# Loads of a mixture-of-experts layer: every second weight tile of the later experts issued from ScalarE's queue

## The chip, the cores and the metric

The kernel runs on one core of a Trainium2 chip. The metric is the device time of one execution in microseconds (us). TensorE (PE) multiplies, VectorE (DVE) and ScalarE (ACT) do elementwise work, GpSimd (POOL) does little here, and SyncE (SP) computes nothing: it issues loads and stores. ACT issues a few small loads as well. Each engine takes its instructions strictly in order, and a load is such an instruction: if its semaphores aren't there yet, all that stands behind it on that engine waits too.

## The reference, cut to what matters

One layer over 256 tokens of width 2048: a projection, two recurrent branches, a gated merge and a layer norm, then a mixture of experts in which each of 16 experts picks its 32 best tokens, and a second layer norm.

```
aff = softmax(h @ w_router)                       # 256 x 16
gate, idx = top_k(aff.T, 32)                      # per expert
xe  = h[idx]                                      # 16 x 32 x 2048
hid = silu(xe @ w1) * (xe @ w3)                   # w1, w3: 16 x 2048 x 1024
eo  = (hid @ w2) * gate                           # w2: 16 x 1024 x 2048
out = layer_norm(alpha * h + scatter_add(idx, eo))
```

All is float32. The three expert weights are 16 x 3 x 8 MB, each read once.

## The kernel before, in words

**Stages.** The projections and recurrences come first and are laid out by hand in one long interleaved order. The experts follow in four groups of four (`for gq in range(4)`, L1454). For each expert of a group PE runs the up product: 16 tiles of w1 and w3, taken in pairs, each tile 128 partitions x 2048 floats, which is 1 MB (L1469). ACT and DVE then form silu times gate: two ACT instructions on the result (L1479, L1480), four on DVE, four PE transposes (L1487) and one ACT copy (L1489), which writes the tile `hid`. After the fourth expert the down product runs over 32 tiles of w2, four (one per expert) for each of eight blocks of rows (L1518). At its end four `eo` copies on ACT (L1525), each behind the last matmul of its quarter of the columns, feed a product that scatters the rows back (L1528) and is added up on DVE. In the last group the final two blocks of rows are cut by columns into five stripes of 4 tiles, three of 512 KB a tile and two of 256 KB. Each group but the first begins with a gather: PE picks the tokens (L1388), DVE and ACT write them, half and half (L1395, L1393).

**The order of the loads.** The list `order` holds all 396 weight tiles in the order of their use: per group 64 of w1 and w3, then those of w2. `prefetch()` issues the next one, and `take()` hands out the next one. Tile 64 is the first w2 tile of the first group. The first 24 tiles are loaded early, into whatever buffers are free. From tile 24 on the buffers go round in a cycle of 18: nine `ring_a`, two `t8b`, seven `ring`. A tile's buffer is thus free when the tile some 18 places earlier has been multiplied.

**What sets the order of instructions.** Up to the end of the first expert (`region.close()`, L1474) it is as written. Behind that a scheduler places each engine's instructions by its own model of times. It also gives each load one of eight completion semaphores in turn (DMAHW0 to 7), over all engines together. A load first waits for the load that had the same semaphore before it, that is, for the one eight places earlier in the order in which loads were placed. So at most eight weight loads are under way at a time. In the kernel before all of these loads stand on SP (L135).

Of the kernel before, what the change touches and what calls it, by code (L numbers as in the profile page):

```python
# [54 lines left out]
def build(tc, x, w_in, gla_a_up_f, gla_a_bias_f, gla_a_up_b, gla_a_bias_b, gla_norm_g,  # L55
# [3 lines left out]
    nc = tc.nc  # L59
# [26 lines left out]
    def S(shape, tag, bufs=1, dt=F32):  # L86
        return (mid if tag in ("t8", "t8b", "x16") else sp if tag in main_tags else cp).tile(shape, dt, tag=tag, name=tag, bufs=bufs)
# [23 lines left out]
    def prefetch(halves=False):  # L111
        i = len(issued)
        if i < len(first):
            slot = first[i]
            i = use.index(slot) + first[:i].count(slot)
        else:
            slot = again[(i - len(first)) % len(again)]
        ap = order[i]
        shape = list(ap.shape)
        if slot == "a":  # L120
            t = ring_a[0].tile(shape, F32, tag="ring_a", name="ring_a", bufs=NRA)
        elif slot == "x":
            if not pair:
                both = S([128, 2, 2048], "x16", 2)
                pair.extend((both[:, 0], both[:, 1]))
            t = pair.pop(0).rearrange("p (k f) -> p k f", k=shape[1])
        elif slot == "t":
            t = S(shape, "t8b", 2)
        elif slot == "p":
            t = ring_p[0].tile(shape, F32, tag="ring_p", name="ring_p", bufs=NRP)  # L130
        else:
            t = ring_b[0](shape)
        issued[i] = t
        if not halves:
            nc.sync.dma_start(t, ap)  # L135
            return None
        n = shape[1] // 2
        nc.sync.dma_start(t[:, 0:n], ap[:, 0:n])
        return lambda: nc.sync.dma_start(t[:, n:], ap[:, n:])

    def take():
        while taken[0] not in issued:
            prefetch()
        taken[0] += 1
        return issued[taken[0] - 1]
# [1110 lines left out]
    def all_chains():  # L1256
# [38 lines left out]
        chain_pool.close()  # L1295
        ring_a.append(st.enter_context(tc.tile_pool(name="ra", bufs=1, side="left", reuse_waits="tile")))
        early.extend([lambda: prefetch(True)] * NRA)
        yield from load_y(0, "x16", 2)
        yield from merge_t()

    run_chain(all_chains())
    early.extend([lambda: prefetch(True)] * (NRX + NRT))
    need("out4")
    while early:
# [291 lines left out]
```

## Time and profile before

| | |
|---|---|
| median of 3 runs | 1819.86 us (1819.25 to 1820.95) |
| the profiled execution | 1819.94 us |
| its span, first to last instruction | 1818.2 us |
| PE busy | 88% of the span |
| DVE, ACT busy | 43%, 30% |
| mean granted TensorE clock | 0.962 |

Shares over the whole span mix two stages. In the first, up to about 850 us, PE, DVE and ACT are all busy; in the second, the experts, the DMA engines are. A row of the sliced view has 40 digits or numbers, one for each 45.5 us.

### The profile page before, as it was taken

To read this page: it belongs to the slowest core of one execution; us is meant where nothing else is said; L and a number is where in the kernel's file an instruction comes from. 1 tells how busy PE (TensorE), PEld (TensorE's weight loads), DVE (VectorE), ACT (ScalarE), POOL (GpSimd) and SP (SyncE) were. 2 spreads that over 40 slices of the span, in tenths; PEclk is the share of its full clock that TensorE was granted. 3 is DMA by queue.
4 is the path that set the end of the run, shared out by engine and by line. 5 is a ranking of instruction groups with operands and counts; after the bars stand their busy time and mean duration, and the time that the engine had idled before them with its cause. 6 is when DMAs were issued, how large, how long until landed. Compare 5 with 4: busy or idle time off the path is not lost.

```text
span 1818.2 us, 27708 instructions
## 1 busy us (share of the span) xinstructions
PE 1600.9 (88%) x11255; PEld 955.3 (53%) x11255; DVE 773.4 (43%) x1400; ACT 548.6 (30%) x1081; POOL 16.5 (1%) x42
## 2 busy tenths in 40 slices
PE   8999999999999999999776997668986679966696
PEld 8998897798777788889421232112331113411132
DVE  6778776777568866655321211111031110111104
ACT  5566454564566755444200000000010000100001
POOL 0000000000000000000000000000000000000000
PEclk9999999999999999999899999889999899998998
DMA  7757374654655668887999999999999999999997
GB/s 215 236 165 196 106 196 118 180 145 137 176 180 174 191 192 287 301 294 255 399 414 420 420 421 420 421 421 421 421 420 421 421 420 421 421 420 420 411 413 249
DMA packets 203113, 561.84 MB, mean 309 GB/s; under 512 B 49804, under 2 KB 100422, under 8 KB 156522
## 3 DMA queue, kind: packets, MB, share of 16 engines
q1 hardware_dynamic: 185008, 557.70, 81.8%
q10 hardware_dynamic: 17978, 2.37, 0.8%
q8 instruction: 88, 1.44, 0.3%
q14 instruction: 39, 0.32, 0.0%
HBM read 543.24 MB, written 16.78 MB: 308 GB/s over the span
## 4 chain that ended last, share of the span: by engine, by line
DMA 40%; PE 39%; DVE 5%; ACT 2%; issue 1%; SPq 0%; ACTq 0%; DVEq 0%
DMA ring<-in_w_dram 18%; DMA ring_a<-in_w_dram 17%; PE mm L284 7%; PE mm L285 6%; PE mm L286 6%; PE mm L1518 5%; DMA t8b<-in_w_dram 4%; PE mm L1469 2%; PE mm L275 2%; PE mm L277 1%; PE mm L276 1%; PE ax L1170 1%; DVE wlo L65 1%; DVE t L65 1%; ACT whi L238 1%
## 5 line engine op out<-in xcount | busy, mean ns | idle before, releaser
L65 DVE TENSOR_TENSOR wlo<-wraw,whi 128x512 fp32r<-128x512 f32 (+2 forms) x480 | 310.9, 664 | 179.1 <-ACT whi L238 173.4
L238 ACT ACTIVATE whi<-wraw 128x512 fp32r<-128x512 f32 (+2 forms) x480 | 283.8, 609 | 147.1 <-PE mm L286 61.1
L275 PE MATMUL mm<-x,whi 128*128 128x256 f32 x688 | 206.9, 301 | 2.9 <-ACT whi L238 2.9
L1469 PE MATMUL mm<-ring_a,x 128*32 128x512 f32 x776 | 156.0, 675 | 55.9 <-DMA ring_a<-in_w_dram 55.9
L277 PE MATMUL mm<-x,wlo 128*128 128x256 f32 x688 | 194.4, 283 | 0.8 <-issue 0.8
L276 PE MATMUL mm<-x,whi 128*128 128x256 f32 x688 | 194.7, 283 | 0.0
L1481 DVE TENSOR_SCALAR sig<-sig 64x512 f32<-64x512 f32 x16 | 6.8, 424 | 433.9 <-ACT sig L1479 433.9
L1518 PE MATMUL mm<-ring_a,hid 128*32 128x512 f32 (+1 forms) x524 | 164.0, 598 | 1.3 <-ACT sig L1479 1.3
L284 PE MATMUL mm<-whi,x 128*128 128x512 f32 x384 | 162.8, 424 | 0.0
L1469 PE MATMUL mm<-ring,x 128*32 128x512 f32 x592 | 117.5, 679 | 49.9 <-DMA ring<-in_w_dram 49.9
L285 PE MATMUL mm<-wlo,x 128*128 128x512 f32 x384 | 153.2, 399 | 0.0
L286 PE MATMUL mm<-whi,x 128*128 128x512 f32 x384 | 152.8, 398 | 0.0
L65 DVE TENSOR_TENSOR x<-x,ax 128x512 f32<-128x512 f32 (+1 forms) x34 | 22.2, 655 | 271.4 <-PE ax L1528 271.4
L275 PEld LDWEIGHTS mm<-x,whi 128*128 128x128 f32 x688 | 131.0, 190 | 12.3 <-issue 5.1
L276 PEld LDWEIGHTS mm<-x,whi 128*128 128x128 f32 x688 | 131.1, 191 | 2.9 <-issue 2.9
L1479 ACT ACTIVATE sig<-mm 64x512 f32<-64x512 f32 x16 | 9.4, 588 | 406.4 <-PE mm L1469 406.4
L277 PEld LDWEIGHTS mm<-x,wlo 128*128 128x128 f32 x688 | 131.0, 190 | 0.3 <-DVE wlo L65 0.3
L1518 PE MATMUL mm<-ring,hid 128*32 128x512 f32 x392 | 125.3, 594 | 1.3 <-ACT sig L1479 0.7
L1469 PEld LDWEIGHTS mm<-ring_a,x 128*32 128x32 f32 x776 | 30.1, 116 | 158.1 <-DMA ring_a<-in_w_dram 105.9
L1518 PEld LDWEIGHTS mm<-ring_a,hid 128*32 128x32 f32 x524 | 46.6, 111 | 111.2 <-issue 95.1
L1525 ACT ACTIVATE eo<-mm 128x512 f32<-128x512 f32 (+1 forms) x17 | 9.7, 572 | 294.2 <-PE mm L1518 281.3
L1469 PEld LDWEIGHTS mm<-ring,x 128*32 128x32 f32 x592 | 22.7, 117 | 133.0 <-DMA ring<-in_w_dram 92.3
(348 smaller groups left out, 2134.6 us busy)
## 6 DMA issues: line engine op xcount, KB each, us to landing
ring_a<-in_w_dram SPq DMA_DIRECT2D x180, 1024.0 KB
ring<-in_w_dram SPq DMA_DIRECT2D x139, 1024.0 KB
wraw<-in_w_in_dram SPq DMA_DIRECT2D x112, 512.0 KB
t8b<-in_w_dram SPq DMA_DIRECT2D x39, 1024.0 KB
wraw<-in_w_in_dram SPq DMA_DIRECT2D x96, 256.0 KB
wraw<-in_w_out_dram SPq DMA_DIRECT2D x24, 512.0 KB
ring_a<-in_w_dram SPq DMA_DIRECT2D x22, 512.0 KB
wraw<-in_w_up_rwkv_dram SPq DMA_DIRECT2D x16, 512.0 KB
```

The lines of the kernel that those rows point to most:

```text
L65: dve.tensor_tensor(out_, a, b, op=op)
L238: act(hi, raw, AF.Copy)
L275: mm(o, whi[:, sl], hi(k), start=(st0 and cb % 2 == 0), stop=False, skip_group_check=True)
L276: mm(o, whi[:, sl], lo(k), start=False, stop=False, skip_group_check=True)
L277: mm(o, wlo[:, sl], hi(k), start=False, stop=st1, skip_group_check=True)
L284: mm(o, hi(k)[:, sl], whi, start=st0, stop=False)
L285: mm(o, hi(k)[:, sl], wlo, start=False, stop=False)
L286: mm(o, lo(k)[:, sl], whi, start=False, stop=st1)
L1170: mm(pv[:, h, j, :], ke[:, h, j * 128:j * 128 + 128], qe[:, h, iq * 128:iq * 128 + 128], start=True, stop=True)
L1469: mm(ps[32 * q:32 * q + 32, :], xe[:, kb, e4 * 32:e4 * 32 + 32], wt[q // 2][:, k, (q % 2) * 512:(q % 2) * 512 + 512], start=(kb == 0), sto ...
L1518: mm(pss[c // 512][32 * e4:32 * e4 + 32, c % 512:c % 512 + m], hids[e4][:, fb % 4, fb // 4, :], wt[e4][:, j, c - c0:c - c0 + m], start=(fb ...
L1525: act(eo[:, 0:m], pss[c // 512][:, c % 512:c % 512 + m], AF.Copy)
```

## The change

From tile 64 on, a tile with an odd number is issued by ACT instead of SP. These are 166 of the 332 loads from there. All first loads, the small ones and the stores stay where they were.

```
         issued[i] = t
         if not halves:
-            nc.sync.dma_start(t, ap)
+
+            (nc.scalar if i >= 64 and i % 2 else nc.sync).dma_start(t, ap)
             return None
```

The new blank line moves all lines behind it by one (L1479 becomes L1480). As the scheduler places the rest, it also changes the order of loads and a few matmuls. In the rows below a tile has its buffer's name and a serial number; what a row waits for stands in brackets, and the same number on two engines is the same tile.

**ACT, end of the first group.** Before: the last three experts' instructions, and the four `eo` copies of the down product.

```order
L1489 ACTIVATE hid_10962<-ax_10957 128x256 [waits PE_49]
L1479 ACTIVATE sig_11061<-mm_10964 64x512 [waits DVE_49,PE_49]
L1480 ACTIVATE h1_11062<-mm_10964 64x512
L1489 ACTIVATE hid_11074<-ax_11069 128x256 [waits PE_49]
L1479 ACTIVATE sig_11173<-mm_11076 64x512 [waits DVE_49,PE_49]
L1480 ACTIVATE h1_11174<-mm_11076 64x512
L1489 ACTIVATE hid_11186<-ax_11181 128x256 [waits PE_49]
L1525 ACTIVATE eo_11418<-mm_11222 128x512 [waits PE_49]
L1525 ACTIVATE eo_11426<-mm_11223 128x512 [waits PE_49]
L1525 ACTIVATE eo_11434<-mm_11224 128x512 [waits PE_49,Activation_49]
L1525 ACTIVATE eo_11442<-mm_11225 128x512 [waits PE_49,Activation_49]
```

Now, from the same `hid_11074` on:

```order
L1490 ACTIVATE hid_11074<-ax_11069 128x256 [waits PE_49]
L136 DMA t8b_11252<-in_w2_dram 128x2048 [waits DMAHW3_49,DMAHW5_49,DMAHW1_49,DMAHW7_49,DMAHW0_49,PE_49]
L136 DMA ring_11256<-in_w2_dram 128x2048 [waits DMAHW5_49,DMAHW7_49,DMAHW0_49,PE_49]
L136 DMA ring_a_11228<-in_w2_dram 128x2048 [waits DMAHW3_49]
L1480 ACTIVATE sig_11173<-mm_11076 64x512 [waits DVE_49,PE_49]
L1481 ACTIVATE h1_11174<-mm_11076 64x512
L136 DMA ring_a_11232<-in_w2_dram 128x2048 [waits DMAHW5_49,DMAHW1_49]
L1490 ACTIVATE hid_11186<-ax_11181 128x256 [waits PE_49]
L136 DMA ring_11276<-in_w2_dram 128x2048 [waits DMAHW1_49]
L136 DMA ring_11280<-in_w2_dram 128x2048 [waits DMAHW3_49]
L136 DMA ring_11300<-in_w2_dram 128x2048 [waits DMAHW5_49,Activation_49]
L136 DMA t8b_11352<-in_w2_dram 128x2048 [waits DMAHW7_49,PE_49]
```

Tile 69 (`t8b_11252`) and tile 71 (`ring_11256`) stand before tile 65 (`ring_a_11228`), and tile 67 (`ring_a_11232`) between two of the expert's steps; tile 87 (`t8b_11352`) comes ahead of tile 79, which is the row behind the last. Tile 87 takes the buffer of tile 69 and so waits for PE.

**SP, the same place.** Before, tiles 64 to 72 in the order of use:

```order
L135 DMA ring_a_11226<-in_w2_dram 128x2048 [waits DMAHW0_49]
L135 DMA ring_a_11228<-in_w2_dram 128x2048 [waits DMAHW1_49]
L135 DMA ring_a_11230<-in_w2_dram 128x2048 [waits DMAHW2_49]
L135 DMA ring_a_11232<-in_w2_dram 128x2048 [waits DMAHW3_49]
L135 DMA ring_a_11250<-in_w2_dram 128x2048 [waits DMAHW4_49]
L135 DMA t8b_11252<-in_w2_dram 128x2048 [waits DMAHW5_49]
L135 DMA t8b_11254<-in_w2_dram 128x2048 [waits DMAHW6_49]
L135 DMA ring_11256<-in_w2_dram 128x2048 [waits DMAHW7_49,PE_49]
L135 DMA ring_11274<-in_w2_dram 128x2048 [waits DMAHW0_49,PE_49]
```

Now, from tile 64 (`ring_a_11226`) on:

```order
L136 DMA ring_a_11226<-in_w2_dram 128x2048 [waits DMAHW2_49]
L136 DMA ring_a_11230<-in_w2_dram 128x2048 [waits DMAHW4_49]
L136 DMA ring_a_11250<-in_w2_dram 128x2048 [waits DMAHW6_49]
L136 DMA t8b_11254<-in_w2_dram 128x2048 [waits DMAHW7_49]
L136 DMA ring_11274<-in_w2_dram 128x2048 [waits DMAHW0_49,PE_49]
L136 DMA ring_11278<-in_w2_dram 128x2048 [waits DMAHW2_49,PE_49]
L136 DMA ring_11298<-in_w2_dram 128x2048 [waits DMAHW4_49,PE_49]
L136 DMA ring_a_11302<-in_w2_dram 128x2048 [waits DMAHW6_49,PE_49]
L136 DMA t8b_11370<-in_w2_dram 128x2048 [waits DMAHW7_49,DMAHW0_49,PE_49]
L136 DMA ring_a_11322<-in_w2_dram 128x2048 [waits DMAHW2_49]
L136 DMA ring_11374<-in_w2_dram 128x2048 [waits DMAHW4_49,PE_49]
L136 DMA ring_a_11326<-in_w2_dram 128x2048 [waits DMAHW6_49]
```

The even tiles are left. From tile 78 (`ring_a_11302`) on near and far ones alternate: 78, 88, 80, 90, 82. Each far one waits for PE to have used the tile whose buffer it takes.

**ACT, between two experts of the second group.** `ring_11705` is the last tile of its second expert, and `sig_11715` the first step behind that expert's matmuls. Before: no load stands here.

```order
L1479 ACTIVATE sig_11603<-mm_11450 64x512 [waits PE_49]
L1480 ACTIVATE h1_11604<-mm_11450 64x512
L1489 ACTIVATE hid_11616<-ax_11611 128x256 [waits PE_49]
L1479 ACTIVATE sig_11715<-mm_11618 64x512 [waits DVE_49,PE_49]
L1480 ACTIVATE h1_11716<-mm_11618 64x512
L1489 ACTIVATE hid_11728<-ax_11723 128x256 [waits PE_49]
```

Now:

```order
L136 DMA ring_11693<-in_w3_dram 128x2048 [waits DMAHW6_49]
L136 DMA ring_11705<-in_w3_dram 128x2048 [waits DMAHW0_49]
L136 DMA ring_11733<-in_w3_dram 128x2048 [waits DMAHW2_49]
L136 DMA ring_11745<-in_w3_dram 128x2048 [waits DMAHW4_49]
L1480 ACTIVATE sig_11715<-mm_11618 64x512 [waits DVE_49,PE_49]
L1481 ACTIVATE h1_11716<-mm_11618 64x512
L136 DMA ring_a_11757<-in_w3_dram 128x2048 [waits DMAHW5_49]
L136 DMA ring_a_11769<-in_w3_dram 128x2048 [waits DMAHW7_49]
L1490 ACTIVATE hid_11728<-ax_11723 128x256 [waits PE_49]
L136 DMA ring_a_11781<-in_w3_dram 128x2048 [waits DMAHW1_49]
L136 DMA ring_a_11793<-in_w3_dram 128x2048 [waits DMAHW3_49]
L136 DMA t8b_11805<-in_w3_dram 128x2048 [waits DMAHW5_49]
```

At `sig_11715` four loads have been issued in a row, two of them for the next expert; two more stand between its steps.

**ACT, the last stripes.** Before, the five `eo` copies stand together:

```order
L1525 ACTIVATE eo_13627<-mm_13463 128x512 [waits PE_49]
L1525 ACTIVATE eo_13657<-mm_13464 128x512 [waits PE_49]
L1525 ACTIVATE eo_13687<-mm_13465 128x512 [waits PE_49,Activation_49]
L1525 ACTIVATE eo_13717<-mm_13466 128x256 [waits PE_49,Activation_49]
L1525 ACTIVATE eo_13745<-mm_13466 128x256 [waits PE_49,Activation_49]
```

Now:

```order
L1526 ACTIVATE eo_13627<-mm_13463 128x512 [waits PE_49]
L136 DMA ring_a_13673<-in_w2_dram 128x2x512 [waits DMAHW1_49]
L136 DMA ring_a_13677<-in_w2_dram 128x2x512 [waits DMAHW3_49]
L1526 ACTIVATE eo_13657<-mm_13464 128x512 [waits PE_49]
L136 DMA ring_a_13703<-in_w2_dram 128x2x256 [waits DMAHW5_49]
L136 DMA ring_a_13707<-in_w2_dram 128x2x256 [waits DMAHW7_49]
L136 DMA t8b_13731<-in_w2_dram 128x2x256 [waits DMAHW1_49]
L136 DMA ring_13735<-in_w2_dram 128x2x256 [waits DMAHW3_49,DMAHW2_49]
L1526 ACTIVATE eo_13687<-mm_13465 128x512 [waits PE_49,Activation_49]
L1526 ACTIVATE eo_13717<-mm_13466 128x256 [waits PE_49,Activation_49]
L1526 ACTIVATE eo_13745<-mm_13466 128x256 [waits PE_49,Activation_49]
```

The odd tiles of the third stripe wait behind the `eo` copy of the first, those of the last two stripes behind that of the second.

## Rows read from the trace of the kernel before

**Rows 1.** The page's slices: DMA engines' busy tenths, and GB/s moved.
```profile
DMA  7757374654655668887999999999999999999997
GB/s 215 236 165 196 106 196 118 180 145 137 176 180 174 191 192 287 301 294 255 399 414 420 420 421 420 421 421 421 421 420 421 421 420 421 421 420 420 411 413 249
```

**Rows 2.** Windows: length, busy by engine, clock, DMA share, GB/s in the last column.
```profile
880.00:900.00 20.00, 15.51 (x107) 8.73 (x108) 6.80 (x18) 2.29 (x5) 0.00 (x0) 0.76 1.01 417
940.00:960.00 20.00, 11.95 (x67) 2.24 (x65) 2.35 (x2) 1.07 (x2) 0.00 (x0) 1.00 1.01 424
1000.00:1700.00 700.00, 564.78 (x2545) 164.06 (x2543) 96.36 (x111) 34.52 (x70) 0.00 (x0) 0.94 1.01 421
```

**Rows 3.** The chain that ended last, two of its pieces: start, length, what.
```profile
1015.61 19.92 DMA ring_a<-in_w_dram
...
1115.50 19.85 DMA ring_a<-in_w_dram
```

**Rows 4.** What SP waited for, 1000 to 1700 us: total, times, longest.
```profile
SPq L135 <- DMA ring_a<-in_w_dram: 292.0, 139, 3.1
SPq L135 <- DMA ring<-in_w_dram: 230.1, 109, 3.1
...
SPq L135 <- PE mm L1518: 1.4, 5, 0.3
```

**Rows 5.** SP at line L135: ns of one issue (min/median/max), start times.
```profile
L135 SPq DMA_DIRECT2D ring_a<-in_w_dram x140: 327/328/328, 1013.1 to 1698.4; - x140
```

**Rows 6.** SP's timeline: start, length, queue, loads merged; one cycle of buffers.
```profile
1057.96 20.26 SPq L135 DMA_DIRECT2D ring_a<-in_w_dram  x9
...
1102.78 20.54 SPq L135 DMA_DIRECT2D ring_a<-in_w_dram  x9
```

**Rows 7.** ACT's timeline, end of group one, an expert of group two.
```profile
997.70 0.59 ACT L1479 ACTIVATE sig<-mm 64x512 f32<-64x512 f32 x1 [33.69 <-PE mm L1469]
...
1004.27 0.38 ACT L1489 ACTIVATE hid<-ax 128x256 f32<-128x256 f32 x1 [5.50 <-PE ax L1487]
1076.61 1.33 ACT L1525 ACTIVATE eo<-mm 128x512 f32<-128x512 f32 x2 [71.95 <-PE mm L1518]
...
1117.44 0.59 ACT L1479 ACTIVATE sig<-mm 64x512 f32<-64x512 f32 x1 [15.57 <-PE mm L1469]
1117.93 0.58 ACT L1480 ACTIVATE h<-mm 64x512 f32<-64x512 f32 x1
1124.02 0.38 ACT L1489 ACTIVATE hid<-ax 128x256 f32<-128x256 f32 x1 [5.51 <-PE ax L1487]
```

**Rows 8.** PE's timeline around the first down product, and the end of an expert.
```profile
995.75 1.91 PE L1469 MATMUL mm<-ring_a,ring 128*32 128x512 f32 x12 [1.44 <-DMA ring_a<-in_w_dram]
...
1004.17 7.50 PE L1429 MATMUL ax<-lnrow,ident 16*128 16x512 f32 x14
1011.59 1.07 PE L1518 MATMUL mm<-ring_a,hid 128*32 128x512 f32 x2
...
1024.04 11.50 PE L1518 MATMUL mm<-ring,hid 128*32 128x512 f32 x50
...
1115.48 1.91 PE L1469 MATMUL mm<-ring,x 128*32 128x512 f32 x12 [1.35 <-DMA ring<-in_w_dram]
```

**Rows 9.** A window in the last group, where ACT loads rows of ln2.
```profile
1720.00:1735.00 15.00, 14.70 (x55) 4.55 (x55) 7.34 (x9) 4.66 (x8) 0.00 (x0) 1.00 0.96 367
```

**Rows 10.** What ACT waited for, 1700 to 1760 us: a small load's landing.
```profile
ACT sig L1507 <- DMA h<-in_ln_b_dram: 5.1, 3, 2.1
```

**Rows 11.** The tail on ACT: first, second and last `eo` copy of five.
```profile
1783.90 0.60 ACT L1525 ACTIVATE eo<-mm 128x512 f32<-128x512 f32 x1 [48.26 <-PE mm L1518]
1789.29 0.60 ACT L1525 ACTIVATE eo<-mm 128x512 f32<-128x512 f32 x1 [4.79 <-PE mm L1518]
...
1801.23 0.38 ACT L1525 ACTIVATE eo<-mm 128x256 f32<-128x256 f32 x1 [2.31 <-PE mm L1518]
```

**Rows 12.** The tail on SP: its last weight load.
```profile
1792.83 0.37 SPq L135 DMA_DIRECT2D ring<-in_w_dram  x1
```

**Rows 13.** DMA queues, 1000 to 1818 us: packets, MB, share of 16 engines.
```profile
q1 hardware_dynamic: 51168, 335.03, 99.3%
...
q10 hardware_dynamic: 40, 0.04, 0.0%
```

## The prediction

> **What bounds the kernel now.** The sliced view comes first. From the 20th slice on, about 865 us, the DMA engines are at nine tenths or more and move 399 to 421 GB/s until the last slices [rows 1]. A window says it more sharply: from 1000 to 1700 us they move 421 GB/s at a share of 1.01, while PE is busy for 565 of 700 us [rows 2]. At that rate a 1 MB tile (1.049 MB) takes 2.49 us. SP's timeline agrees: the same nine buffers come round after 1102.78 - 1057.96 = 44.82 us, and 44.82 / 18 tiles = 2.49 us [rows 6]. The chain of waits consists of pieces of 19.85 to 19.92 us, each from a load's issue to its landing [rows 3]. That is 8 x 2.49 = 19.9, so eight loads are always under way, as many as there are semaphores. SP waits 292 and 230 us for such landings, but 1.4 us for the down product's matmuls [rows 4], so a tile's buffer is free well before its turn.
>
> Two things do not bound it. One issue takes SP 0.328 us [rows 5], 13% of the 2.49. And PE is quicker than the loads: when it had tiles in store it did 50 matmuls of the down product in 11.50 us, 0.23 each, so four, one tile, take 0.92 us [rows 8]. The experts' time is bytes over rate, and then a tail. The change can act in three ways only: by another rate, by leaving the DMA engines without work, or in the tail.
>
> **The change part by part.**
>
> *Issuing.* 166 issues of 0.328 us, 54 us in all, move to ACT. ACT mostly waits (33.69 us before one expert's first step, 71.95 us before the first `eo`) [rows 7], and SP does not need the relief. I take 0.
>
> *Rate.* The 332 loads from tile 64 on hold 335.5 MB (335.03 on SP's queue q1 from 1000 us on, almost the same stretch) and 0.04 MB on ACT's queue q10 [rows 13]. 335.5 / 421 is 797 us. Two queues with large loads at once stand nowhere in this trace. The nearest rows are full windows of one queue: the best, 424 GB/s, gives 791.3 us (-5.6), the worst, 417, gives 804.6 (+7.7) [rows 2]. I take 421, the 700 us that the change is made in: 0.
>
> The Trainium skill speaks against a gain here: "DMA: Bandwidth & Descriptors", section "Rules for kernel authors", says that spreading loads over several issuing engines does not help bandwidth, since all of them run on the same 16 DMA engines, and only saves issue time. By that rule this term is 0. The share of 1.01 with one queue agrees with it; that two queues move no more, no run here shows yet.
>
> *ACT behind PE, between experts.* ACT now stands at `sig_11715` with its next loads behind it, until PE has used that expert's last tile, `ring_11705`. From that landing on: 1.91 us of matmuls [rows 8], then the two ACT steps of 0.59 and 0.58 us [rows 7], some 3.3 us with what lies between, until ACT issues again. The next block, at the expert's `hid`, lasts until 1124.02 - 1117.44 = 6.6 us after the first step [rows 7], and two loads are issued before it. Under way beyond `ring_11705` are the two of ACT that stand ahead of `sig_11715` and SP's own, about four of the eight: 6 x 2.49 = 14.9 us of work against 3.3. Covered: 0. SP's loads hide it, and where SP is stopped too the cover ends.
>
> *The start of the down product, where both can stop.* SP stands at tile 88 until PE has used tile 70, ACT at 87 until PE has used 69. Before, tile 63 had landed at 995.75 and PE came back to the down product at 1011.59, after 7.50 us of broadcasts from 1004.17 on [rows 8]. Now tiles 69 and 71 are loaded out of turn, ahead of 65. That makes 64 and 65 up to 2 x 2.49 = 5.0 us late, and PE's return too: 1016.6. Tiles 64 to 71 then take 8 x 0.92 = 7.4 us, so both queues move again by 1024. With 64 landing at 995.75 + 3 x 2.49 = 1003.2, the twelve loads after it up to 78 (69 and 71 are done) last until 1003.2 + 12 x 2.49 = 1033. Margin 9 us: 0. Later in each down product a far tile goes ahead of a near one, 2.49 us of delay each time, which PE makes up at 0.92 us a tile.
>
> *Gathers.* ACT's eight gather steps now stand between loads that wait for landings, so PE follows the loads in a group's first expert instead of catching up in one go. 18 buffers less 8 under way leave 10 tiles, 25 us, of room: 0.
>
> *The ln2 rows.* From 1720 to 1735 us the rate is 367 [rows 9]: 15 x (1 - 367/421) = 1.9 us are lost already, because ACT's small loads take semaphores in the same turn and wait for ACT's steps. With weight loads between them this can go (-1.9) or happen twice more (+3.8). I take 0, the row as it is.
>
> *Tail.* The third stripe's odd tiles follow the first `eo` (1783.90) and those of the last two the second (1789.29) [rows 11]. Four issues of 0.33 behind a copy of 0.60 end at 1789.29 + 0.60 + 1.3 = 1791.2, before SP's last issue of today, 1792.83 [rows 12]. So the loads are not later. But far before near also holds here, and one tile of 512 KB out of turn puts the first copies back by 1.25 us; PE has more left to do when the last piece lands. Bounds 0 and +5.0 (one stripe of 2.1 MB at 421); I take +1.5, near one piece.
>
> Sum: 1819.94 + 1.5 = 1821.4, made against the profiled execution, which is 0.08 above the median of the runs. A change of this kernel under 0.2%, 3.6 us, can't be told from none.
>
> **The rivals.**
>
> *The queues run dry (slower).* The cover of 9 us at the down product fails: PE uses tiles 69 and 70 later than 1033, for instance because the two queues don't share evenly and tiles 65 and 67 come last. Then both queues stand, and a stop costs at least 2.1 us until a load lands again [rows 10] and 2.49 for its tile: 4.6 us. Four down products make 18.4, time 1839.8; if half of them are hit, 1830.6. For it: ACT is now tied to PE thirteen times by experts' steps and by four rounds of `eo`. Against: the covers above. It decides from a lag of PE of 9 us more than worked out.
>
> *Two queues move more (faster).* 424 GB/s instead of 421, and the loss at ln2 gone: 1821.4 - 5.6 - 1.9 = 1813.9. For it: single windows reach 424. Against: 1.01 of the DMA engines are busy as it is.
>
> The skill's ceiling, "DMA: Bandwidth & Descriptors", section "Where 436 GB/s comes from", is 435 GB/s; by it alone the 335.5 MB would take an estimated 771 us, 26 less. No window of this trace comes near it.
>
> *Two queues move less (slower).* 417 GB/s, as in the slowest full window: 1821.4 + 7.7 = 1829.1. Nothing in this trace speaks for it but that window.
>
> *The change does not act.* The order shows half of the loads on ACT, so this is out.
>
> **How the numbers follow.** Forecast 0.54, dry queues 0.22, more rate 0.15, less rate 0.09. The forecast's own spread, 1818.0 to 1828.7 (tail 0 to +5.0, ln2 -1.9 to +3.8), lies almost wholly within 3.6 us of the median, since both ends together are unlikely. So: faster 0.16, within 0.2% 0.53, slower 0.31. The range runs from 1813, just past the faster rival, to 1838, past the lower rate and most of the dry case.
>
> **What will show it.** Right: q10 carries 166 loads, 168 MB; from 1000 to 1700 us 420 to 422 GB/s; SP now waits for PE at some of its loads, and ACT for landings; PE's return to the first down product 1016 instead of 1011.6; the last `eo` 1 to 3 us later. Wrong: a stretch of the experts below 400 GB/s other than the ln2 rows (dry queues), or another rate all along (one of the two rate rivals).

## The result and the profile after

The changed kernel takes 1835.15 us (median of 4 runs, 1834.36 to 1836.11). The kernel before took 1820.03 us in the same session (4 runs). The ratio is 1.0083, with a 95% interval of 1.0070 to 1.0097: 15 us slower. That lies inside the forecast range. It is not the likeliest case of the prediction, which was "the same", but its first rival, the queues that run dry (1831 to 1840).

The slices come first, the line that answers to [rows 1]: DMA engines' busy tenths and GB/s in 40 slices of the span, and below it the two large queues over the whole program (packets, MB, share of 16 engines).

```profile
DMA  7857373745465668897999999999999999999996
GB/s 212 241 159 200 103 197 113 200 122 169 142 200 171 188 200 282 304 302 265 400 416 421 406 401 420 421 421 421 413 411 421 421 420 422 404 421 421 403 396 217
...
q1 hardware_dynamic: 159824, 389.92, 59.0%
q10 hardware_dynamic: 43162, 170.16, 23.1%
```

Before, every slice from the 22nd on stood at 420 or 421 until the last three. Now the row has dents (406, 401; 413, 411; 404), and between them it is back at 420 to 422. A rate that was lower all along would look different. Queue q10 now carries 170.16 MB, so the split took place.

Windows sharpen this (start and end; length, busy time of PE, of PE's weight loads, of DVE, ACT and GpSimd, granted clock, DMA share, GB/s). The first answers to [rows 2], the last two lie where [rows 9] does.

```profile
1000.00:1700.00 700.00, 488.56 (x2528) 134.41 (x2520) 98.08 (x112) 35.59 (x72) 0.00 (x0) 0.85 1.00 416
1020.00:1040.00 20.00, 19.04 (x106) 4.88 (x104) 3.69 (x6) 0.00 (x0) 0.00 (x0) 0.83 0.96 387
1080.00:1100.00 20.00, 20.00 (x120) 8.13 (x118) 6.07 (x10) 2.85 (x5) 0.00 (x0) 0.96 0.93 376
1320.00:1340.00 20.00, 19.62 (x98) 7.51 (x97) 5.88 (x9) 2.39 (x4) 0.00 (x0) 0.99 0.93 381
1720.00:1740.00 20.00, 12.06 (x67) 2.75 (x67) 5.60 (x5) 1.70 (x3) 0.00 (x0) 0.83 0.97 381
1740.00:1760.00 20.00, 19.27 (x69) 5.51 (x70) 3.89 (x8) 4.66 (x8) 0.00 (x0) 0.74 0.94 375
```

416 instead of 421 over 700 us is 700 x (1 - 416/421) = 8.3 us of DMA time. The dents lie at the start and the end of a down product (1020 and 1080 for the first group, 1320 for the end of the second; the slice with 404 holds the end of the third). The two windows at the ln2 rows lose 1.9 and 2.2 us against 421; before, 1720 to 1740 lost 1.9 and the next window, at 421, nothing.

What SP waited for from 1000 to 1700 us (total, times, longest) answers to [rows 4]:

```profile
SPq L136 <- DMA ring<-in_w_dram: 277.8, 51, 11.7
SPq L136 <- DMA ring_a<-in_w_dram: 216.7, 52, 9.1
SPq L136 <- PE mm L1519: 82.4, 8, 20.2
```

The third line is the news. SP waited 1.4 us for the down product's matmuls before; now 82.4 us, and 20.2 at a time, which is as long as eight loads take. The first such place, on three timelines (start, length, engine; idle time before and its releaser in brackets), ACT first:

```profile
1006.23 0.59 ACT L1480 ACTIVATE sig<-mm 64x512 f32<-64x512 f32 x1 [40.16 <-PE mm L1470]
...
1012.81 2.98 ACTq L136 DMA_DIRECT2D ring<-in_w_dram  x3
1032.15 0.36 ACTq L136 DMA_DIRECT2D t8b<-in_w_dram  x1
```

SP at the same place:

```profile
1013.30 0.33 SPq L136 DMA_DIRECT2D ring_a<-in_w_dram  x1
1032.19 0.33 SPq L136 DMA_DIRECT2D t8b<-in_w_dram  x1
```

And PE, which both wait for; its rows answer to [rows 8]:

```profile
1004.27 1.91 PE L1470 MATMUL mm<-ring_a,ring 128*32 128x512 f32 x12 [0.82 <-DMA ring_a<-in_w_dram]
...
1012.70 8.38 PE L1430 MATMUL ax<-lnrow,ident 16*128 16x512 f32 x14
1021.01 5.33 PE L1519 MATMUL mm<-ring_a,hid 128*32 128x512 f32 x8
1026.27 1.44 PE L1430 MATMUL ax<-lnrow,ident 16*128 16x512 f32 x2
```

From 1015.8 to 1032.15 neither queue issues anything. The loads under way finish, and the rate falls to 387. PE is 8.5 us later than before at the broadcasts (1012.70 against 1004.17), then takes 5.33 us for eight matmuls, and two more broadcasts follow. Only at 1032 has it used the tiles that the two queues stand at.

The tail on ACT, which answers to [rows 11]:

```profile
1796.65 0.60 ACT L1526 ACTIVATE eo<-mm 128x512 f32<-128x512 f32 x1 [37.42 <-PE mm L1519]
...
1804.51 0.60 ACT L1526 ACTIVATE eo<-mm 128x512 f32<-128x512 f32 x1 [7.26 <-PE mm L1519]
...
1815.08 0.38 ACT L1526 ACTIVATE eo<-mm 128x256 f32<-128x256 f32 x1 [2.31 <-PE mm L1519]
```

The last copy comes 13.85 us later than before (1801.23). From the first copy to the last it takes 18.4 us, before 17.3, so the tail itself grew by 1.1 us. The rest came earlier.

The part before the first expert's first step took between 906.5 and 918.4 us in the profiled runs below. Profiles are therefore also compared by the time from that step to the last copy. The step in the kernel before, then in the changed one:

```profile
912.37 0.59 ACT L1479 ACTIVATE sig<-mm 64x512 f32<-64x512 f32 x1
```

```profile
913.07 0.59 ACT L1480 ACTIVATE sig<-mm 64x512 f32<-64x512 f32 x1
```

1801.23 - 912.37 = 888.9 us before, 1815.08 - 913.07 = 902.0 after, 13.1 more.

### The profile page after: what moved, and what is told of

Same layout as the page of the kernel before. It is cut to its first block, busy times and chain, and to the rows that moved or that the text cites. A ratio compares the mean times of both kernels' runs of the same rounds, so it can differ in the third digit from the quotient of the medians.

```text
span 1832.6 us, 27555 instructions
## 1 busy us (share of the span) xinstructions
PE 1523.5 (83%) x11255; PEld 922.8 (50%) x11255; DVE 773.4 (42%) x1400; ACT 548.3 (30%) x1081; POOL 16.5 (1%) x42
## 3 DMA queue, kind: packets, MB, share of 16 engines
q10 hardware_dynamic: 43162, 170.16, 23.1%
## 4 chain that ended last, share of the span: by engine, by line
PE 41%; DMA 38%; DVE 5%; ACT 2%; issue 1%; ACTq 0%; DVEq 0%; SPq 0%
DMA ring_a<-in_w_dram 17%; DMA ring<-in_w_dram 15%; PE mm L285 7%; PE mm L286 6%; PE mm L287 6%; DMA t8b<-in_w_dram 5%; PE mm L1470 4%; PE mm L1519 3%; PE mm L276 2%; PE mm L278 1%; PE mm L277 1%; PE ax L1389 1%; PE ax L1529 1%; DVE sig L1483 1%; PE ax L1430 1%
## 5 line engine op out<-in xcount | busy, mean ns | idle before, releaser
L1470 PE MATMUL mm<-ring_a,x 128*32 128x512 f32 x776 | 139.6, 757 | 71.2 <-DMA ring_a<-in_w_dram 71.2
L1519 PE MATMUL mm<-ring_a,hid 128*32 128x512 f32 (+1 forms) x524 | 138.8, 634 | 26.2 <-DMA ring_a<-in_w_dram 25.6
L1519 PE MATMUL mm<-ring,hid 128*32 128x512 f32 x392 | 118.7, 623 | 32.4 <-DMA ring<-in_w_dram 32.4
L1480 ACT ACTIVATE sig<-mm 64x512 f32<-64x512 f32 x16 | 9.4, 588 | 356.7 <-PE mm L1470 233.3
L1470 PEld LDWEIGHTS mm<-ring_a,x 128*32 128x32 f32 x776 | 26.0, 125 | 152.4 <-DMA ring_a<-in_w_dram 111.1
L1519 PEld LDWEIGHTS mm<-ring_a,hid 128*32 128x32 f32 x524 | 33.4, 116 | 111.0 <-issue 71.3
```

The costliest lines, as they stand in the source:

```text
L1470: mm(ps[32 * q:32 * q + 32, :], xe[:, kb, e4 * 32:e4 * 32 + 32], wt[q // 2][:, k, (q % 2) * 512:(q % 2) * 512 + 512], start=(kb == 0), sto ...
L1519: mm(pss[c // 512][32 * e4:32 * e4 + 32, c % 512:c % 512 + m], hids[e4][:, fb % 4, fb // 4, :], wt[e4][:, j, c - c0:c - c0 + m], start=(fb ...
```

## The experiments

All ratios are to the kernel before, run on the same chip in the same session; the sections stand in the order in which the thinking went.

**Near first.** Each queue keeps its own loads in the order of the tiles; the split is unchanged.

```
-            (nc.scalar if i >= 64 and i % 2 else nc.sync).dma_start(t, ap)
+            q = int(i >= 64 and i % 2)
+            ins = (nc.scalar if q else nc.sync).dma_start(t, ap)
+            if i >= 64:
+                if q in last_load:
+                    follow(ins, last_load[q])      # order only, no semaphore
+                last_load[q] = ins
```

> The changed kernel, with one thing taken out: on each of the two queues the weight loads now stand in the order of their tiles, so that no load that must wait for a use by TensorE stands ahead of the load of a nearer tile. The loads are still split by halves between SyncE and ScalarE, and ScalarE's loads still stand behind its expert steps. Theory 'order' (far loads ahead of near ones stop both queues at once at the start and the end of a down product): the dips of the changed kernel at 1020-1040, 1080-1100, 1320-1340 (387, 376, 381 GB/s) go, SP's waits for the down product's matmuls (82.4 us) fall under 10 us, and the time is 1819 to 1824. Theory 'ScalarE is tied to TensorE' (its loads stand behind waits of its compute steps, whatever their order): the dips stay, SP's ring waits grow, 1830 to 1836. Theory 'two queues move less': below 420 GB/s in all windows and no lower than 1833. Tail and ln2 rows may keep 2 to 5 us in either of the first two.

Measured: 1829.58 us, ratio 1.0056 (1.0037 to 1.0074). Three windows, then SP's waits for the ln2 rows from 1000 us on, then two rows of ACT's timeline:

```profile
1000.00:1700.00 700.00, 494.35 (x2506) 135.46 (x2508) 98.01 (x112) 35.48 (x72) 0.00 (x0) 0.86 1.01 420
1720.00:1740.00 20.00, 15.63 (x71) 4.20 (x72) 6.37 (x6) 2.68 (x5) 0.00 (x0) 0.79 0.81 323
1740.00:1760.00 20.00, 18.16 (x76) 4.79 (x75) 3.63 (x6) 3.68 (x6) 0.00 (x0) 0.78 0.75 299
```

```profile
SPq L142 <- DMA h<-in_ln_b_dram: 26.8, 2, 22.6
```

```profile
1730.97 0.59 ACT L1490 ACTIVATE sig<-mm 64x512 f32<-64x512 f32 x1 [33.90 <-PE mm L1480]
...
1744.18 0.28 ACTq L1516 DMA_DIRECT2D h<-in_ln_b_dram  x1
```

The dents at the down products are gone: 420 over the 700 us. In that the order was their cause. But only 5 of the 15 us came back, by the median of the runs; the profiled execution (1831.43 us) needs 900.9 us from the first expert's first step to the last copy, 1.1 less than the changed kernel. Some 6.6 us less are lost from 1000 to 1700 us, and 6.4 more at the ln2 rows, 4.7 and 5.8 us in the two windows. There SP waits 22.6 us in one piece for a small load that ACT issues at 1744.18. ACT issues it behind the first step of the last expert and the steps that follow; that step comes at 1730.97 us, 13 us later than before (1717.88), although nearly all bytes up to 1700 us moved at the old rate. SP's waits for the down product's matmuls fell to 43.4 us and not under 10, as "order" had it: the waits stayed without a dent. So PE is late without any loss of rate: other tiles had landed than the ones it needed. Each theory had one half: "order" the rate, "ScalarE is tied to TensorE" the time, which lies 0.4 us under its range. That PE is late at a full rate stood in neither.

**Drift.** How far SP is ahead of ACT can be read from the queues' bytes. Two windows of 20 us of the near-first kernel, 1480 to 1500 us and 1540 to 1560 us (packets, MB, share):

```profile
q1 hardware_dynamic: 671, 4.86, 58.6%
q10 hardware_dynamic: 482, 3.54, 42.5%
```

```profile
q10 hardware_dynamic: 783, 5.66, 68.2%
q1 hardware_dynamic: 381, 2.73, 32.8%
```

PE uses the tiles in turn, one of SP's and one of ACT's. In the first window SP gets (4.86 - 3.54)/1.049 = 1.3 tiles ahead; in the second, in the down product, ACT makes up 2.8. Summed from 880 us on (q1's MB less the other queue's, in tiles; the level comes from the tiles below 64, only the changes count):

```
until us            1060  1160  1240  1300  1420  1500  1580  1700
changed             46.4  46.6  47.7  48.3  48.8  47.9  46.9  48.8
near first          46.7  47.4  48.9  46.4  49.3  51.4  48.0  50.8
on GpSimd           45.2  45.2  45.2  45.2  45.2  45.2  45.2  45.3
tied by eight       42.3  43.2  45.7  45.7  45.7  45.6  45.6  45.7
tied by four        48.4  48.4  48.4  48.4  48.5  48.5  48.6  48.7
tie alone           47.4  45.8  48.3  48.3  48.2  48.2  49.5  46.0
```

In the near-first kernel SP's lead rises by up to 5 tiles within a group's experts (46.4 to 51.4). A tile is 2.49 us, so 4 to 5 tiles are 10 to 12.5 us, the size of PE's delay there. In the changed kernel the lead rises by only 2.4 at these points, and its last expert's first step is as late (820.4 us after the first expert's, 819.6 in the near-first kernel, 805.5 before). So the lead does not give the size of the delay by itself; what it does, the tie below tests. ACT's timeline shows how it comes about: at the last expert's first step, ACT has issued only one load beyond the tiles that this step waits for; the rest stands behind it.

The Trainium skill describes what happens then: by "DMA: Bandwidth & Descriptors", section "Queues, rings and completion order", each DMA engine takes turns between the queues that have work. Windows of the kernel tied by four (below), with both queues full, agree, at 4.2 MB each in 20 us; where ACT stands, SP takes its turns, as in the first window above.

**Only w1 and w3 on ACT; only w2 on ACT.** The condition gets a third part, `up` or `not up`:

```
+            up = i % 96 < 64 if i < 288 else i < 352
-            (nc.scalar if i >= 64 and i % 2 else nc.sync).dma_start(t, ap)
+            (nc.scalar if i >= 64 and i % 2 and up else nc.sync).dma_start(t, ap)
```

> The changed kernel with only the odd tiles of w1 and w3 on ScalarE's queue; every w2 tile is back on SyncE. Theory 'order at the down product': at the start of a down product SP still holds its near and far tiles mixed, but ScalarE has only far ones (the next experts'), so about half of the dips go: 1821 to 1828. Theory 'ScalarE is tied to TensorE': ScalarE's expert steps lie just where these tiles are loaded, so most of the loss stays: 1829 to 1836. Both: the tail of the last two stripes is as in the kernel before, so the last first copy comes within 2 us of 1783.9 plus what was lost until then.

> The changed kernel with only the odd tiles of w2 on ScalarE's queue; w1 and w3 are back on SyncE. Theory 'order at the down product': the far-before-near pairs of w2 (87 and 88 ahead of 79, 105 and 106 ahead of 99) stand as in the changed kernel, so most of the 15 us stays: 1828 to 1836. Theory 'ScalarE is tied to TensorE at the experts' steps': no load stands between these steps any more but those of w2 at the end of a group, so most of the loss goes: 1820 to 1825. If this one and the one with w1 and w3 alone lose 5 to 9 us each, the loss is spread over both sorts of places and belongs to the mere split.

Measured: w1 and w3 alone 1828.25 us, ratio 1.0048 (1.0029 to 1.0067); w2 alone 1822.18 us, 1.0025 (1.0014 to 1.0036). Windows of the first:

```profile
1000.00:1700.00 700.00, 540.12 (x2528) 154.38 (x2520) 97.98 (x112) 35.59 (x72) 0.00 (x0) 0.89 1.01 420
1720.00:1740.00 20.00, 12.39 (x60) 3.22 (x53) 6.37 (x6) 2.68 (x5) 0.00 (x0) 0.84 0.74 301
```

And one of the second:

```profile
1020.00:1040.00 20.00, 16.15 (x103) 4.37 (x100) 1.29 (x2) 0.00 (x0) 0.00 (x0) 0.90 0.94 384
```

The time of the first, 1828.25, lies between the two ranges, 0.25 us above that of "order" and 0.75 under the other's, so it decides nothing. The rows do: the larger loss comes with w1 and w3, without a dent at any down product, and is the late step (1731.66 us) and the ln2 rows again. With w2 alone the first dent is there (384), but the later ones are not, and the time, 1822.18, lies in the range of "ScalarE is tied to TensorE" and 6 us under that of "order".

**On GpSimd.** The near-first edit with `nc.gpsimd` in the place of `nc.scalar`.

> Odd tiles from tile 64 on are issued by GpSimd instead of ScalarE, in tile order on each queue as in the near-first run. GpSimd has next to no work among the experts, and its loads have semaphores of their own, so more than eight loads can be under way. Theory 'order': no better than the near-first run, 1818 to 1824. Theory 'ScalarE is tied to TensorE': this one is 1818 to 1824 while the near-first run stays above 1829. Theory 'eight loads under way are what sets 421 GB/s': the rate rises above 424 in windows with both queues full, and the time falls to 1805 to 1815. A cost of issuing on GpSimd that no trace shows yet would make it slower than the near-first run at a full rate.

Measured: 1836.46 us, ratio 1.0104 (1.0086 to 1.0121). SP's waits from 1000 to 1700 us, then three windows, then GpSimd's loads in the tail:

```profile
SPq L142 <- PE mm L1480: 361.7, 89, 11.2
```

```profile
1000.00:1700.00 700.00, 483.29 (x2576) 131.04 (x2576) 98.54 (x112) 35.58 (x72) 72.74 (x137) 0.85 1.01 419
1020.00:1040.00 20.00, 20.00 (x55) 5.83 (x57) 10.30 (x16) 0.00 (x0) 1.06 (x2) 0.61 0.91 369
1780.00:1800.00 20.00, 11.66 (x44) 2.60 (x40) 5.02 (x10) 1.19 (x2) 3.50 (x5) 0.83 0.52 181
```

```profile
1786.90 0.71 POOL L142 DMA_DIRECT2D ring<-in_w_dram  x1 [6.20 <-issue]
1791.07 0.72 POOL L142 DMA_DIRECT2D ring<-in_w_dram  x1 [3.46 <-PE mm L1529]
1795.21 0.70 POOL L142 DMA_DIRECT2D ring_a<-in_w_dram  x1 [3.42 <-issue]
```

With GpSimd, which has no compute steps among the experts, there is no drift: 45.2 tiles throughout. SP now mostly waits for PE's use of a buffer and not for landings, and the rate is still 419 to 421 in full windows. By the times of the issues and the bytes that the queues had still to move, 1.2 more loads were under way on the mean than in the kernel before, and in the near-first kernel 1.8 fewer, at the same rate. So, within these counts, the number of loads under way did not set the rate. The kernel is slow for other reasons. In the tail GpSimd issues one piece of 512 KB every 4.1 to 4.2 us from 1786.90 on (the two before it were 7 us apart), and the rate falls to 181: from the first copy to the last it takes 28.1 us, before 17.3. What GpSimd waits for there the profile shows for some of these loads only, and the cause stays open. And the last expert's first step comes 8 us later than in the kernel before (813.6 us after the first expert's), with a dent of 2.5 us at the start of the first down product (369). So an even lead alone does not bring the step back, and why it is late here stays open too.

**The ln2 rows moved, in the kernel before and in the near-first one.** Their eight small loads go to GpSimd's queue.

```
-                nc.scalar.dma_start(raw[0:3], ln2_g[:, sl].broadcast_to([3, 512]))
-                nc.scalar.dma_start(raw[3:5], ln2_b[:, sl].broadcast_to([2, 512]))
+                nc.gpsimd.dma_start(raw[0:3], ln2_g[:, sl].broadcast_to([3, 512]))
+                nc.gpsimd.dma_start(raw[3:5], ln2_b[:, sl].broadcast_to([2, 512]))
```

> The kernel before, all weights on SyncE's queue, with one edit: the eight small loads of the ln2 rows go to GpSimd's queue instead of ScalarE's. In the kernel before they cost 367 GB/s over 15 us, 1.9 us [rows 9]. Theory 'shared semaphores' (SyncE's next weight load must wait until a small load that stands behind ScalarE's steps has landed): SyncE no longer waits for those rows, the stretch runs at 419 to 421, and the time is 1.0 to 2.5 us under the kernel before. Rival 'the small loads themselves are what takes the time': the stretch stays at 360 to 380 and the time is the same.

> The near-first kernel (both queues in tile order, 420 GB/s from 1000 to 1700 us, 323 and 299 GB/s from 1720 to 1760) with the ln2 rows on GpSimd's queue. Theory 'shared semaphores': the loss of 10.5 us at the ln2 rows falls under 3 and the time is 1820 to 1824. Theory 'drift' (ScalarE loses turns while it stands at an expert's step, SyncE goes ahead by up to 4 or 5 tiles, and TensorE then lacks ScalarE's tiles): TensorE still comes 10 to 13 us late to the last group's down product, so buffers come free late and most of the 10 us only moves into the tail, 1825 to 1830.

Measured: the kernel before with this edit 1817.35 us, ratio 0.9996 (0.9982 to 1.0009); near first with it 1822.88 us, 1.0026 (1.0014 to 1.0038). One window of each, the kernel before first (it answers to [rows 9]):

```profile
1720.00:1735.00 15.00, 13.41 (x31) 3.81 (x30) 6.20 (x9) 4.54 (x8) 3.08 (x6) 0.66 1.02 420
```

```profile
1720.00:1740.00 20.00, 15.85 (x60) 4.48 (x61) 6.38 (x6) 4.60 (x9) 2.27 (x4) 0.84 0.91 350
```

420 instead of 367: the row's dent comes from semaphores that SP's loads share with loads standing on ACT, not from the small loads. The 1.9 us that it gives can't be told in the run times. In the near-first kernel the loss at the ln2 rows falls from 10.5 to 3.4 us and the ratio by 0.0030, 5.5 us, although the last expert's first step is as late as before (821.2 us after the first expert's, 819.6 in the near-first kernel, 805.5 in the kernel before). So of the near-first kernel's loss some 5 us went with the shared semaphores, and as much again stays while PE is late (each to within 4 us or so, by the ratios' intervals). That the part which stays is the price of PE's delay is argued from the late step and not shown by itself.

**Tied.** The near-first kernel; ACT's first step of each expert from the fourth on, and its copies, now stand behind its load of the eighth tile after those they wait for.

```
+    def ahead(op, last):
+        while last + 8 not in issued:
+            prefetch()
+        follow(op, last_load[1])
...
-            act(sg_[up_], ps[lo_], AF.Exp, scale=-1.0)
+            first_step = act(sg_[up_], ps[lo_], AF.Exp, scale=-1.0)
+            if e >= 3:
+                ahead(first_step, 96 * gq + 16 * e4 + 15)
```

The copies `eo` of the first three groups get the same line with `96 * gq + 95`. The loop also brings SP's loads up to that tile forward in the program, so the edit changes more than ACT's order.

> The near-first kernel with the drift taken out: each expert's first step on ScalarE, from the fourth expert on, and the copies at the end of the first three down products stand behind ScalarE's load of the eighth tile after the one they wait for, so that ScalarE always has its half of the eight loads under way when it stands. Theory 'drift': SyncE's lead over ScalarE stays within 1.5 tiles from 1060 to 1700 us (it went up by 4 in the near-first run), the last expert's first step comes at 1717 to 1721 us as in the kernel before (1717.9; 1731.0 in the near-first run), the ln2 rows lose 2 to 4 us instead of 10.5, and the time is 1819 to 1824. Rival 'drift is a by-product' (TensorE is late because of its lower clock in short bursts): the step stays near 1730 and the time at 1828 to 1831 though the lead is even. What stays above the kernel before is the tail.

> Both edits at once: queues tied as in the tied kernel, and the ln2 rows on GpSimd's queue. If drift and the shared semaphores are the whole of the loss but the tail, the rate is 419 to 421 GB/s in every window from 1000 to 1780 us and the time is 1817 to 1821, 0 to 2 us under the tied kernel. If something else in the split costs time (the clock of TensorE, the tail with the eight last half-size loads behind copies on ScalarE), it stays 3 us or more above the kernel before with a full rate until 1780.

Measured: tied 1819.12 us, ratio 1.0003 (0.9992 to 1.0014); with the ln2 rows moved as well 1821.61 us, 1.0019 (1.0007 to 1.0031). Of the tied kernel two windows and the last expert's first step:

```profile
1000.00:1700.00 700.00, 476.13 (x2556) 131.64 (x2550) 98.34 (x112) 34.82 (x72) 0.00 (x0) 0.84 1.01 421
1720.00:1740.00 20.00, 11.92 (x33) 3.54 (x30) 6.37 (x6) 3.99 (x8) 0.00 (x0) 0.67 1.02 422
```

```profile
1720.42 0.59 ACT L1495 ACTIVATE sig<-mm 64x512 f32<-64x512 f32 x1 [20.84 <-PE mm L1485]
```

The whole loss is gone with half of the loads still on ACT. The step is at 1720.42 instead of 1730.97 (811.4 us after the first expert's instead of 819.6; 805.5 in the kernel before), the ln2 rows lose next to nothing, and the lead holds at 45.6 to 45.7 from 1240 us on. It rose by 3.4 tiles before that, which the expectation excluded, at no cost in rate. From 1000 to 1700 us the granted clock is 0.84 (a mean between the levels of 1.2 and 2.4 GHz) against 0.94 before, and the time is the same, so the lower clock is not what costs. With the ln2 rows moved too, no gain was found; its 3.5 us over the kernel before have no dent in its profile to answer to. That is the second case of its expectation, that something else in the split costs time; the other tied kernels don't show it, and it stays open.

**Half the tie, and the tie alone.** `last + 4` instead of `last + 8`; and the tie of eight without the `follow` between loads.

> The tied kernel with half of the tie: the same steps of ScalarE stand behind its load of the fourth tile after the one they wait for instead of the eighth, so ScalarE has two loads under way when it stands instead of four. Theory 'drift': something between the near-first kernel (first step of the last expert 1731.0, ratio 1.0056) and the tied one (1720.4, 1.0003): SyncE's lead rises and falls again by 1 to 2 tiles within a group, the step comes at 1722 to 1727, the ln2 rows lose 2 to 7 us, and the time is 3 to 7 us over the kernel before. If any tie does (the order of the steps alone matters), it is the tied kernel's time within 2 us.

> The tied kernel without the edges that keep each queue in tile order; far loads stand ahead of near ones again at the start of a down product, though fewer than in the changed kernel, since the tie also sets some of the order. Theory 'order' as a cause of its own: a dip to 390 GB/s or less comes back at one or more of the down products and the time is 4 to 9 us over the kernel before. Theory 'drift alone' (far loads only hurt because ScalarE had too few loads under way when it stood): no dip below 410 from 1000 to 1700 us and a time within 3 us of the kernel before.

Measured: tied by four 1820.36 us, ratio 1.0000 (0.9989 to 1.0012); tie alone 1824.54 us, 1.0030 (1.0014 to 1.0045). Of the tie alone one window, and what SP waited for from 1000 to 1700 us:

```profile
1020.00:1040.00 20.00, 20.00 (x96) 5.75 (x98) 7.99 (x13) 0.00 (x0) 0.00 (x0) 0.77 0.92 366
```

```profile
SPq L142 <- PE mm L1534: 52.7, 7, 15.9
```

Half the tie does all: the lead is 48.4 to 48.7 throughout. The middle value that theory "drift" expected was wrong, and the other reading, that any tie does, gave the time; two loads of ACT beyond those that the step waits for were enough here. Without the tile order the first down product is dry again and SP waits 52.7 us for PE at such places (82.4 in the changed kernel).

Together the runs make a square, ratios to the kernel before:

```
                      far loads first      tile order
loads behind steps        1.0083             1.0056
loads ahead (tie)         1.0030             1.0003
```

By the runs, the order of tiles is worth 0.0027 in either row and the tie 0.0053 in either column, some 5 us and 10 us. Each ratio is uncertain by 0.0011 to 0.0018, so each difference by about 0.002: that they agree to the last digit is chance. The four profiled executions, from the first expert's first step to the last copy, take 13.1, 12.0, 6.7 and 1.1 us more than the kernel before, in the order in which the square is read; there the order is worth 1.1 us behind the steps and 5.6 ahead of them. So there are two causes, and each costs time with the other removed; how they add up is not settled. With both removed the split costs nothing that can be measured in the two tied kernels, apart from the open 3.5 us of the third. No version beat the kernel before.

## Why the prediction was right in its range and wrong in its mechanism, point by point

The range, 1813 to 1838, holds the 1835.15 us, but the sum of 1821.4 lies 13.7 us under it: the terms that were put at 0 were not 0. What brought the time into the range is the rival of the dry queues, which had been given 0.22, and that is partly luck. This rival's price for one place was too high, and that made up for 5.5 us that lie elsewhere. The forecast's own spread, 1818.0 to 1828.7, was said to lie almost wholly within 3.6 us of the median; half of it lies above that.

- **Issuing, rate: right.** Full windows of every two-queue kernel stand at 419 to 424 GB/s, as with one queue. The rule of the Trainium skill that was weighed ("DMA: Bandwidth & Descriptors", section "Rules for kernel authors": several issuing engines don't add bandwidth) is now borne out by these rows; both rate rivals fall.
- **The start of the down product: wrong, the step that failed first.** It put PE's return at 1016.6 us and left a margin of 9 us. It counted tiles 69 and 71 as a delay of tiles 64 and 65 only. Tile 63 itself was late: the last matmuls before the expert's first step came at 1004.27 instead of 995.75. ACT's loads had taken DMA time ahead of it, 3.2 MB by 1000 us, three tiles or 7.5 us. PE was back at 1021.01. The next tiles were priced at 0.92 us each, 7.4 in all, and took from 1021.0 to 1032. Both queues then stood until 1032.15. The rival named this place and this mechanism. Its price was too high for one place (4.6 us; 1.6 to 2.1 measured). Its count of four was right, but only the first place is the start of a down product. The other three are the ends of the first three down products, where tile 105 goes out ahead of 99 on ACT and 106 ahead of 100 on SP (in the first, ACT's `t8b` at 1084.06 us before its `ring_a` at 1084.43); the dents there (376, 381) are the deeper ones. The prediction had named far tiles ahead of near ones there, as a delay of 2.49 us that PE makes up, and not as a stop of both queues.
- **ACT behind PE between experts: wrong in its conclusion.** It said that SP's loads hide ACT's stand, and the rate is indeed full there. What was missed is that the bytes which hide it are not the next ones that PE needs. A full DMA queue was taken for progress. It was also read from one place, where two of ACT's loads beyond the expert's tiles stand ahead of the step; at five of the thirteen steps, the last three among them, it is one. 0 was taken; the tie, of these steps and of the `eo` copies together, gives back some 10 us, to within 4.
- **The ln2 rows: within their bounds.** 0 was taken, with bounds of -1.9 to +3.8; it was 2.2 us more in the changed kernel. In the near-first one it was 8.6, beyond them. The small loads stand behind a step of ACT that waits for PE, so PE's delay goes into this price.
- **Gathers:** no run isolates them; the tied kernels have them between loads too and run at the full rate, so 0 holds there.
- **Tail:** +1.5 taken, +1.1 measured between the first and the last copy.
- **The signals:** 168 MB on q10, right (167.8 more than before's 2.37); SP waiting for PE, right; 420 to 422 GB/s, wrong (416); PE's return, wrong by 4.4 us; the last copy 13.85 us later and not 1 to 3.

Of the 13.85 us, 8.3 are the rate from 1000 to 1700 us, 2.2 more are lost at the ln2 rows, 1.1 in the tail, and 0.7 was there at the first expert's step. The other 1.5 are not assigned.

## What to carry to other kernels

Before loads are split over two queues, ask of each queue what stands in it ahead of the next tile that the consumer needs: a compute step that waits for that consumer, or a load whose buffer the consumer has yet to free. A full DMA rate doesn't show that the right bytes are moving; compare the bytes by queue, and the time at which the consumer reaches a fixed step. If an engine with compute steps must issue loads, have some of them (two were enough here) under way before each step that waits, and keep every queue in the order of use.

## What the runs showed of the hardware that was not expected

- The number of loads under way did not set the rate in the range that occurred: 1.2 more on the mean than in the kernel before with half on GpSimd, and 1.8 fewer in the near-first kernel, at 419 to 421 GB/s in full windows.
- In the tail GpSimd issued pieces of 512 KB only every 4.1 to 4.2 us at best, against 1 MB every 4.98 us in step with SP at the full rate shortly before (1753.70 to 1758.68 us).
- A granted clock of 0.84 instead of 0.94 from 1000 to 1700 us left the time unchanged (tied kernel). PE was busy for 476 us there, before for 565.
